# First SwiGLU of a two-layer trunk: one plain block and five pairs, in the order of the inner SwiGLUs

## The chip, the core and the metric

One core of a Trainium2 chip. Its engines run side by side, each through its own instructions in their written order: TensorE (PE; its weight loads are shown apart as PEld) multiplies, VectorE (DVE) and ScalarE (ACT) work element by element, GpSimd (POOL) does that too and issues loads that add to what is already in the buffer ("accumulating loads"), SyncE (SP) issues plain loads. Engines wait for one another by semaphores. SBUF is the memory that all of them read; TensorE writes its sums to PSUM. The metric is the device time of one execution in microseconds (us).

## What is computed

512 tokens of 1024 values go through two layers. Each layer adds half a SwiGLU, then a mixing of attention and convolution, then half a second SwiGLU; a last norm ends it. All in float32. The change is in the very first SwiGLU, the one that begins with the input:

```python
def rms_norm(x, gain):
    inv = lax.rsqrt(jnp.mean(xf * xf, axis=-1, keepdims=True) + NORM_EPS)
    return (xf * inv).astype(x.dtype) * gain

def swiglu(h, w_gate, w_up, w_down):
    return (jax.nn.silu(h @ w_gate) * (h @ w_up)) @ w_down

for l in range(DEPTH):                                   # DEPTH = 2
    x = x + 0.5 * swiglu(rms_norm(x, ffn1_norm[l]), ...)  # w_gate, w_up: 1024 x 2816
    ...                                                   # mixing
    x = x + 0.5 * swiglu(rms_norm(x, ffn2_norm[l]), ...)  # w_down: 2816 x 1024
return rms_norm(x, final_norm)
```

## The kernel before

**Products in three parts.** float32 accuracy comes from splitting each operand into a rounded part and a remainder (hi and lo) and multiplying hi·hi, hi·lo, lo·hi, all summed in PSUM. A weight piece of 512 KB ("unit", tile `raw`) is loaded, ScalarE casts it to `wh` (line 235), VectorE subtracts to get `wl` (line 236). There are eight `raw` tiles and four each of `wh` and `wl`. `need_split` runs the splits up to three units ahead of TensorE and the loads four or more ahead.

**Blocks.** The 2816 hidden columns are 11 blocks of 256. A block can be done *plain*: gate and up for it, 96 products of 128x512. Two blocks can be done as a *pair* by Strassen-Winograd's scheme with seven products in place of eight (`winograd2`): with the tokens cut in four quarters b11, b12, b21, b22 (by halves of the model width and of the tokens), the operands are b11, b21, t2, t3, t1, t4, b22 in this order (table `CHAINS`), where t3 = b12 - b22, t2 = t3 - b11, t1 = b11 - b12, t4 = t2 + b21. Each comes with its combination of weights: a11, a12, s2 = a11 + s1, s3, s1, a22, s4. s1 and s3 are sums of two pieces, made by an accumulating load on GpSimd (line 230); s2 and s4 are added on VectorE (lines 266 and 291). A pair is 168 products. Its results come out turned (tokens by columns), are cut into 16-bit planes by ScalarE, turned back by transposing loads and put together again. A *single* block ("u", `winograd`, line 1162 for its products) is done by the same scheme on half-width products, 168 of 128x256. Down projections are plain for one block ("d", 48 products) or shared over four or five blocks by the same scheme ("s").

**Stages.** A SwiGLU is a list of stages. The first one had its own list: plain blocks 0 and 1, down of 0, pair 2 and 3, down of 1, pairs 4/5, 6/7, 8/9, single 10, shared down of 2 to 5, shared down of 6 to 10. The three inner ones: plain block 0, pair 1/2, down of 0, pairs 3/4, 5/6, 7/8, 9/10, shared down of 3 to 6, down of 1, shared down of 7 to 10 and 2.

**The start.** The first SwiGLU has no norm ahead of it that could be hidden. `First.take` turns the tokens and multiplies them by the gain only; the plain block is computed from these unscaled tokens (`h`), and the scale of each token, `inv`, comes in at the gate (lines 1029 and 1031), when its sums of squares are done. Meanwhile `copy_x` keeps the turned tokens unsplit in `xs`; `First.scale` (line 552, eight VectorE steps) multiplies them by gain and `inv`, and `Seven` makes the pairs' operands from them: adds on VectorE (lines 745 to 751), then a split. Those were spread over plain block 1 and the first down stage.

**Order.** The engines' instructions stand in the order in which the code issues them, apart from what a scheduler moves by priorities; `tc.issue_after` and `behind` hold an instruction behind another. Each engine keeps its order at run time: an instruction that waits holds up everything behind it.

Of the kernel before, what the change touches and what calls it, by code (L numbers as in the profile page):

```python
# [39 lines left out]
)  # L40
LAST = INNER[:-3] + (("s", (1, 3, None)), ("s", (5, 7, None)), ("d", (9, 10)))
# [30 lines left out]
PAIRS = ((0, 1), (2, 3), (4, 5), (6, 7), (8, 9))  # L72
THREES = ((0, 1, 2), (3, 4, 10), (5, 6, 8), (7, 9, 13), (11, 12, 14))
# [9 lines left out]
def trunk_kernel(  # L83
# [161 lines left out]
    def need_split(g):  # L245
        while state["split"] <= min(g, len(order) - 1):
# [6 lines left out]
            elif isinstance(what, tuple):  # L253
# [3 lines left out]
                if at is PAIRS:  # L257
# [10 lines left out]
            else:  # L268

                need_raw(u + 4 + LOAD_AHEAD)  # L270
                a11, a12, s1, s3, a22 = (raw_of.get(u + i) for i in range(5))
                if what == "s2":
                    nc.vector.tensor_add(a11, a11, s1)
                if what == "s4":
                    nc.vector.tensor_add(a11, a11, a12)
                raw = {"a11": a11, "a12": a12, "s2": a11, "s3": s3, "s1": s1, "a22": a22, "s4": a11}[what]
                if what == FORMS[-1]:
                    for i in range(5):
                        del raw_of[u + i]
# [136 lines left out]
    def plan():  # L416
# [5 lines left out]
        def up(wg, wu, b):  # L422
            top, low = ((w, k, KC // 2, 2 * b * P, 2 * P) for w, k in ((wu, 0), (wu, KC // 2)))
            first = (wg, 0, KC // 2, 2 * b * P, 2 * P)
            u = add_unit(first)
            add_unit((wg, KC // 2, KC // 2, 2 * b * P, 2 * P))
            add_unit(top, low)
            add_unit(top, first)
            add_unit(low)
            order.extend((u, what) for what in FORMS)  # L430

        def seven(at, how, wide=2):
# [4 lines left out]
            place = PAIRS if wide == 2 else THREES_EARLY if how == "early" else THREES  # L437
            for n in range(5 * wide):
# [5 lines left out]
        def ffn(wg, wu, wd, stages):  # L444
            for what, b in stages:
# [7 lines left out]
                if what == "u":  # L453
                    up(wg, wu, b)
                if what == "w":
                    seven(
                        lambda o, j, h: ((wg, wu)[o], KC // 2 * j + 2 * h, 2, 2 * b * P, S), None
# [53 lines left out]
    class First:  # L511


        def __init__(self):
            self.h = [None] * KC
            self.inv = None
            self.xs = [g8(f"xs_{n}", F32, (P, KC // 2, S)) for n in range(2)]

        def take(self, c, src):

            g = par[:, c : c + 1]
            if c % 2 == 0:
                self.pair = both(f"h_{c}", shape=(P, 2, 2, S))
            hi, lo = (t[:, c % 2, :] for t in self.pair)
            self.h[c] = (hi, lo)
# [22 lines left out]
        def scale(self):  # L548

            for c in range(KC):  # L550
                x_ = self.xs[c // 4][:, c % 4, :]
                nc.vector.scalar_tensor_tensor(
                    x_, x_, par[:, c : c + 1], self.inv, op0=ALU.mult, op1=ALU.mult
                )
            self.seven = Seven(self.xs, room_stock, "0")
# [1270 lines left out]
```

## Time and profile before

| | |
|---|---|
| Time, median of 3 | 1633.95 us (1630.48 to 1635.71) |
| The profiled execution | 1633.97 us, of which 1632.2 us from its first to its last instruction (the span) |
| Busy in the span | TensorE 1621.6, VectorE 1315.4, ScalarE 1151.2, GpSimd 203.6 us |
| HBM read | 266.10 MB, 164 GB/s over the span |
| DMA queues' packets | 49.1% of 16 engines' span for the plain loads, 30.1% for GpSimd's |

The page counts an engine as busy while one of its instructions runs. The chain of waits is followed back from the last instruction to whatever released each one. Views of single instructions give the start, the duration, engine and line, what is written and read, and in brackets the idle time ahead of it and what ended it. Products run through the array in a pipeline: their rows last 0.39 us, but they follow one another at 0.2267 us (24 of 128x512 in 5.44 us), and it is this pace that counts.

### The profile page before, as it was taken

The page shows a single profiled execution, that of the slowest core. Times are in us where ns is not written, and L with a number is a line of the kernel's source. Part 1 is how long each engine was busy: PE and PEld are TensorE (multiplying, and loading weights), DVE is VectorE, ACT ScalarE, POOL GpSimd, SP SyncE. Part 2 cuts the span into 40 slices and gives each one's busy share as a digit, 9 for nine tenths or more (in the row PEclk, how much of TensorE's full clock was granted, in tenths as well). Part 3 has the DMA queues.
Part 4 walks back from the last instruction along what each step waited for, and adds up shares of the span by engine and source line. Part 5 has one row for each costly group of instructions (what it writes and reads, how often), then busy time and mean ns, then how long its engine had stood idle before and what let it go on. Part 6 is the DMA issues. An engine that isn't in the chain of part 4 may idle for free.

```text
span 1632.2 us, 21149 instructions
## 1 busy us (share of the span) xinstructions
PE 1621.6 (99%) x7526; PEld 1351.2 (83%) x7526; DVE 1315.4 (81%) x1764; ACT 1151.2 (71%) x1632; POOL 203.6 (12%) x184
## 2 busy tenths in 40 slices
PE   9999999999999999999999999999999999999998
PEld 6888888798888888888888888888988888888886
DVE  7987779977898867698888677988678987778894
ACT  6456777668967667785676777856697775778764
POOL 0011111200111111111101111111002101111111
PEclk9999999999999999999999999999999999999999
DMA  8379999943695779899857899998258857899991
GB/s 253 88 201 208 226 218 238 243 132 78 170 217 130 206 190 223 214 223 280 203 125 207 206 219 219 222 275 199 65 110 223 184 131 196 211 220 232 219 270 56
DMA packets 298702, 315.48 MB, mean 193 GB/s; under 512 B 117316, under 2 KB 181348, under 8 KB 298596
## 3 DMA queue, kind: packets, MB, share of 16 engines
q1 hardware_dynamic: 253188, 230.88, 49.1%
q0 software_dynamic: 44704, 82.59, 30.1%
q8 instruction: 59, 0.97, 0.2%
q10 hardware_dynamic: 704, 0.66, 0.1%
q14 instruction: 47, 0.39, 0.1%
HBM read 266.10 MB, written 2.10 MB: 164 GB/s over the span
## 4 chain that ended last, share of the span: by engine, by line
PE 97%; DVE 1%; DMA 1%; ACT 0%; issue 0%; SPq 0%; ACTq 0%; DVEq 0%
PE x L947 25%; PE y L947 13%; PE x_s L947 10%; PE w L947 6%; PE y_s L947 5%; PE up L1109 4%; PE acc L327 4%; PE acc L328 4%; PE acc L330 4%; PE down L394 4%; PE w_s L947 2%; PE acc L371 2%; PE x_m L947 2%; PE y_m L947 1%; PE z_s L947 1%; PE xt L671 1%
## 5 line engine op out<-in xcount | busy, mean ns | idle before, releaser
L236 DVE TENSOR_TENSOR wl<-raw,wh 128x1024 fp32r<-128x1024 f32 (+2 forms) x510 | 607.0, 1196 | 215.0 <-ACT wh L235 211.0
L235 ACT CAST wh<-raw 128x1024 fp32r<-128x1024 f32 (+2 forms) x510 | 520.2, 1026 | 298.7 <-PE y L947 38.5
L947 PE MATMUL y<-wh,ft 128*128 128x512 f32 x608 | 187.3, 389 | 0.0
L947 PE MATMUL x<-wh,ft 128*128 128x512 f32 x608 | 187.3, 389 | 0.0
L947 PE MATMUL x<-wh,fb 128*128 128x512 f32 x608 | 187.3, 389 | 0.0
L947 PEld LDWEIGHTS x<-wh,fb 128*128 128x128 f32 x608 | 114.2, 188 | 23.6
L947 PEld LDWEIGHTS y<-wh,ft 128*128 128x128 f32 x608 | 114.2, 188 | 23.6
L947 PEld LDWEIGHTS x<-wh,ft 128*128 128x128 f32 x608 | 114.2, 188 | 23.6
L947 PE MATMUL y<-wl,ft 128*128 128x512 f32 x304 | 118.3, 389 | 0.0
L947 PE MATMUL x<-wl,fb 128*128 128x512 f32 x304 | 118.3, 389 | 0.0
L947 PE MATMUL x<-wl,ft 128*128 128x512 f32 x304 | 118.3, 389 | 0.0
L230 POOL DMA_DIRECT2D raw<-in_ffn_wu_dram x39 | 47.0, 1212 | 538.6 <-DMA raw<-in_ffn_wu_dram 268.1
L1284 ACT COPY raw_a<-pt 128x1024 uint16<-128x1024 uint16 x76 | 103.3, 1359 | 13.9 <-DMA pt<-pl 13.8
L327 PE MATMUL acc<-hh,wh 128*128 128x512 f32 x240 | 94.1, 392 | 0.0
L947 PE MATMUL w<-wh,fb 128*128 128x512 f32 x304 | 93.6, 389 | 0.0
L328 PE MATMUL acc<-hl,wh 128*128 128x512 f32 x240 | 93.6, 390 | 0.0
L330 PE MATMUL acc<-hh,wl 128*128 128x512 f32 x240 | 93.5, 390 | 0.0
L947 PE MATMUL x_s<-wh,ft_s 128*128 128x512 f32 x256 | 79.0, 390 | 0.0
L947 PE MATMUL y_s<-wh,ft_s 128*128 128x512 f32 x256 | 78.8, 389 | 0.0
L266 DVE TENSOR_TENSOR raw<-raw,raw 128x1024 f32<-128x1024 f32 (+1 forms) x61 | 72.4, 1191 | 7.0 <-DMA raw<-in_ffn_wd_dram 5.4
L230 POOL DMA_DIRECT2D raw<-in_ffn_wd_dram x38 | 43.5, 1146 | 249.5 <-DVE wl L236 146.7
L230 POOL DMA_DIRECT2D raw<-in_ffn_wg_dram x39 | 46.8, 1215 | 219.5 <-DMA raw<-in_ffn_wu_dram 75.1
(385 smaller groups left out, 3478.2 us busy)
## 6 DMA issues: line engine op xcount, KB each, us to landing
raw<-in_ffn_wu_dram SPq DMA_DIRECT2D x120, 512.0 KB, 5.8
raw<-in_ffn_wd_dram SPq DMA_DIRECT2D x98, 512.0 KB, 7.3
raw<-in_ffn_wg_dram SPq DMA_DIRECT2D x80, 512.0 KB, 5.0
raw<-in_ffn_wu_dram POOLq DMA_DIRECT2D x39, 512.0 KB, 8.5
raw<-in_ffn_wg_dram POOLq DMA_DIRECT2D x39, 512.0 KB, 6.1
raw<-in_w_in_dram SPq DMA_DIRECT2D x36, 512.0 KB, 4.7
raw<-in_ffn_wd_dram POOLq DMA_DIRECT2D x32, 512.0 KB, 8.9
raw<-raw POOLq DMA_DIRECT2D x20, 512.0 KB, 8.0
```

The lines of the kernel that those rows point to most:

```text
L230: nc.gpsimd.dma_start(out=r, in_=rows_of(*more), accum_op=ALU.add)
L235: cast = nc.scalar.copy(hi, raw)
L236: state["sub"] = eng.tensor_sub(lo, raw, f32(hi))
L266: nc.vector.tensor_add(a11, a11, s1)
L327: nc.tensor.matmul(acc, hi[:, k, :], rhs[k][0], start=k == first, stop=False)
L328: nc.tensor.matmul(acc, hi[:, k, :], rhs[k][1], start=False, stop=False)
L330: state["product"] = nc.tensor.matmul(acc, lo[:, k, :], rhs[k][0], start=False, stop=k == last)
L371: nc.tensor.matmul(accs[j][:, t * H : (t + 1) * H], w[:, k, :], x_, start=t + k + i == 0, stop=k == KC - 1 and i == 2, skip_group_check=True,)
L394: nc.tensor.matmul(acc, a[:, k, tok], w[:, k, :], start=i + k + n == 0 and fresh[t], stop=i == last and k == 1 and n == 2, skip_group_chec ...
L947: nc.tensor.matmul(accs[u], x_[:, k if h == 2 else 2 * h + k, tok], w[:, k, :], start=start and h + k + i == 0, stop=h == last and k == wi ...
L1109: nc.tensor.matmul(accs[t], x_[:, tok], w[:, k, :], start=j + k + i == 0, stop=j == 3 and k == 1 and i == 2,)
L1284: nc.scalar.copy(room.rearrange("p c (n z) -> p c z n", z=2)[:, :, z, :], turned[0][:, NT * z + 2 * c : NT * z + 2 * c + 2, :],)
```

## The change

The first SwiGLU takes the inner ones' list of stages: one plain block, then pairs 1/2, 3/4, 5/6, 7/8, 9/10, with the down stages as there. Plain block 1 and the single block 10 become parts of pairs. The pairs take tokens that carry the gain but not the scale: `copy_x` multiplies by the gain, `First.scale` is gone, and the scale of a token, now one number per partition because a pair's results have tokens on partitions, comes in as `y` at the Silu and at the product of gate and up. The operands b11, b21 and b22 are slices of the plain block's own hi and lo tiles, and t1 goes into the fourth slice, that of b12. The adds for t3, t2, t1 and t4 go to GpSimd. In the first pair the units are loaded in another order (`PAIRS_FIRST`), s3 is added on VectorE rather than by a load, and t3, t1 and t4 are made after its steps 0, 1 and 2. The tables of attention biases (`late`) are made after the down stage of block 0 instead of block 1.

```diff
-FIRST = (
-    ("p", 0), ("p", 1), ("d", (0,)), ("w", 2), ("d", (1,)), ("w", 4), ("w", 6), ("w", 8), ("u", 10),
-    ("s", (2, 4, None)), ("s", (6, 8, 10)),
-)
 INNER = (
     ("p", 0), ("w", 1), ("d", (0,)), ("w", 3), ("w", 5), ("w", 7), ("w", 9), ("s", (3, 5, None)),
     ("d", (1,)), ("s", (7, 9, 2)),
 )
+FIRST = INNER[:1] + INNER[1:]
 PAIRS = ((0, 1), (2, 3), (4, 5), (6, 7), (8, 9))
+PAIRS_FIRST = ((0, 1), (4, 5), (2, 3), (6, 7), (8, 9))
...
                 if what == "s2":
                     late = state["late"] if h else None
                     late = state["sub"].ins if h == 2 else late
+                    late = state["gate"].ins if how == "first" else late
                     with tc.issue_after(late) if late else nullcontext():
                         nc.vector.tensor_add(a11, a11, s1)
...
                 if what == "s2" if early else what == "s3":
-                    if how:
+                    if how not in (None, "first"):
                         nc.gpsimd.dma_start(out=a12, in_=a11, accum_op=ALU.add)
                     else:
                         nc.vector.tensor_add(a12, a12, a11)
...
     class First:
...
+            self.y = const.tile([P, NT], F32, name="y")
             self.xs = [g8(f"xs_{n}", F32, (P, KC // 2, S)) for n in range(2)]
+            hs = [
+                [
+                    xpool.tile([P, KC // 2, S], F32R, tag="xf", bufs=8, name=f"h{n}_{o}")
+                    for n in "hl"
+                ]
+                for o in range(2)
+            ]
+            self.h = [tuple(p[:, k, :] for p in hs[o]) for o in range(2) for k in range(4)]
+            self.seven = Seven(self.xs, room_g8, "0", eng=nc.gpsimd)
+            places = {
+                f"b{o + 1}{t + 1}": tuple(p[:, :, t * H : (t + 1) * H] for p in hs[o])
+                for o in range(2)
+                for t in range(2)
+            }
+            self.seven.places["t1"] = places.pop("b12")
+            self.forms.update(places)
...
-        def scale(self):
-            for c in range(KC):
-                x_ = self.xs[c // 4][:, c % 4, :]
-                nc.vector.scalar_tensor_tensor(
-                    x_, x_, par[:, c : c + 1], self.inv, op0=ALU.mult, op1=ALU.mult
-                )
...
             if fresh:
-                nc.vector.tensor_sub(sums[0], b12, b22)
+                self.eng.tensor_sub(sums[0], b12, b22)
             if what == "t2":
-                nc.vector.tensor_sub(sums[1], sums[0], b11)
+                self.eng.tensor_sub(sums[1], sums[0], b11)
             if what == "t1":
-                nc.vector.tensor_sub(b12, b11, b12)
+                self.eng.tensor_sub(b12, b11, b12)
             if what == "t4":
-                nc.vector.tensor_add(sums[1], sums[1], b21)
+                self.eng.tensor_add(sums[1], sums[1], b21)
...
+            eng.tensor_scalar(x_, tps[c], g, None, op0=ALU.mult)
...
+        def forms_on(step):
+            names = {0: ("t3",), 1: ("t1",), 2: ("t4",)}.get(step, ())
+            with behind(state["cast"], state["sub"]):
+                norm.make(*names)
...
+            accs = norm.groups(4, opening)
+            gate(accs[0])
+            gate(accs[1])
+            up(0, accs[2])
+            up(1, accs[3])
+            norm.make("t2")
...
+            def silu(t, src):
+                nc.scalar.activation(
+                    gates[t], src, AF.Silu, scale=1.0 if norm.y is None else by(t)
+                )
+            def times(t):
+                if norm.y is None:
+                    nc.vector.tensor_mul(ups[t], ups[t], gates[t])
+                else:
+                    nc.vector.scalar_tensor_tensor(
+                        ups[t], ups[t], by(t), gates[t], op0=ALU.mult, op1=ALU.mult
+                    )
...
-            if b == (1,) and late:
+            if b == (0,) and late:
                 late()
```

How the order of the instructions moves is shown at two places, both behind the first plain block.

GpSimd, its first instructions after the constants, before (units 12, 13, 16, 17 are weights of pairs 2/3):

```order
L503 MEMSET eps_93 128x1
L230 DMA raw_12_485<-in_ffn1_wu_dram 128x2x512
L230 DMA raw_13_524<-in_ffn1_wu_dram 128x2x512
L230 DMA raw_16_577<-in_ffn1_wg_dram 128x2x512
L230 DMA raw_17_580<-in_ffn1_wg_dram 128x2x512
```

and in the changed kernel (units 8 to 11 are s1 and s3 of pair 1/2; `sums` holds t3 and t2, later t4; `xs` the tokens):

```order
L479 MEMSET eps_93 128x1
L228 DMA raw_8_348<-in_ffn1_wu_dram 128x2x512
L228 DMA raw_9_351<-in_ffn1_wu_dram 128x2x512
L228 DMA raw_10_354<-in_ffn1_wg_dram 128x2x512
L228 DMA raw_11_361<-in_ffn1_wg_dram 128x2x512
L727 TENSOR_TENSOR sums_0_413<-xs_0_96,xs_1_97 128x1024
L729 TENSOR_TENSOR sums_0_413<-sums_0_413,xs_0_96 128x1024
L731 TENSOR_TENSOR xs_0_96<-xs_0_96 128x4x256
L733 TENSOR_TENSOR sums_0_413<-sums_0_413,xs_1_97 128x1024
L228 DMA raw_18_653<-in_ffn1_wu_dram 128x2x512
```

Four adds are new on GpSimd, behind the four accumulating loads of the first pair; the fourth of them waits for VectorE's split of t2 (`ft2`).

VectorE, from the first gate of plain block 0 on, before (`fb` is a split operand, `xs` the tokens that are scaled):

```order
L1029 TENSOR_TENSOR gate_0_0_390<-acc_160,inv 128x512
L1029 TENSOR_TENSOR gate_0_1_394<-acc_200,inv 128x512
L552 SCALAR_TENSOR_TENSOR xs_95<-xs_95,par,inv 128x512 x3
L1031 TENSOR_TENSOR gate_0_0_390<-gate_0_0_390,inv 128x512
L1031 TENSOR_TENSOR gate_0_1_394<-gate_0_1_394,inv 128x512
L552 SCALAR_TENSOR_TENSOR xs_95<-xs_95,par,inv 128x512
L552 SCALAR_TENSOR_TENSOR xs_96<-xs_96,par,inv 128x512 x4
L1038 TENSOR_TENSOR gate_0_0_390<-acc_243,gate_0_0_390 128x512
L1038 TENSOR_TENSOR gate_0_1_394<-acc_360,gate_0_1_394 128x512
L236 TENSOR_TENSOR wl_450<-raw_315,wh_449 128x1024
```

and in the changed kernel, after the same two gates by `inv` of line 1029 (now 1017) and 1031 (now 1019) and the two by `acc`:

```order
L234 TENSOR_TENSOR wl_7_440<-raw_7_316,wh_7_439 128x1024
L234 TENSOR_TENSOR a_0_0_331<-gate_0_0_0_398,a_0_0_331 128x512
L234 TENSOR_TENSOR a_0_0_331<-gate_0_0_1_402,a_0_0_331 128x512
L264 TENSOR_TENSOR raw_4_127<-raw_4_127,raw_8_348 128x1024
L234 TENSOR_TENSOR ft2_0_412<-sums_0_413,ft2_0_412 128x1024
L234 TENSOR_TENSOR ft3_0_459<-sums_0_413,ft3_0_459 128x1024
L234 TENSOR_TENSOR wl_8_468<-raw_4_127,wh_8_467 128x1024
L264 TENSOR_TENSOR raw_5_312<-raw_5_312,raw_9_351 128x1024
L1173 TENSOR_TENSOR gate_0_1_0_502<-w_0_1_0_462,p1_0_1_0_455 128x512
L1173 TENSOR_TENSOR gate_0_1_1_505<-w_0_1_1_463,p1_0_1_1_457 128x512
L234 TENSOR_TENSOR wl_9_487<-raw_5_312,wh_9_486 128x1024
```

The scalings are gone, and the first pair's weights and operands follow at once: wl_8 and wl_9 are the two halves of s2, which meet t2 in the pair's third step. Behind them come the add of raw_4 into raw_6, the split of t1 (`hl_0`) and wl_10 and wl_11, the halves of s3.

More of the change, by code (lines that the diff above doesn't have):

```diff
@@ L437, in seven @@
             place = PAIRS if wide == 2 else THREES_EARLY if how == "early" else THREES
+            place = PAIRS_FIRST if how == "first" else place
             for n in range(5 * wide):
@@ L452, in ffn @@
                         order.append((u, None))
-                if what == "u":
-                    up(wg, wu, b)
                 if what == "w":
                     seven(
-                        lambda o, j, h: ((wg, wu)[o], KC // 2 * j + 2 * h, 2, 2 * b * P, S), None
+                        lambda o, j, h: ((wg, wu)[o], KC // 2 * j + 2 * h, 2, 2 * b * P, S),
+                        "first" if stages is FIRST and b == 1 else None,
                     )
@@ L719, in make @@
                     continue
-                hi, lo = both(f"f{what}_{self.name}")
+                hi, lo = self.places.get(what) or both(f"f{what}_{self.name}")
                 self.forms[what] = (hi, lo)
@@ L757, in room_g8 @@
         return t[:, 0], t[:, 1]
-    def room_stock(name):
-        return [stock(f"sum{n}_{name}", shape=(P, KC // 2, H)) for n in range(2)]
     def room_form(name):
@@ L1211, in apart @@
             def apart(t):
-                if then == "u" and t > 1:
-                    pending.setdefault("u", []).append(lambda: lay(t))
-                else:
-                    lay(t)
-            def lay(t):
                 planes.append(g2(f"pl_{name}_{t}", U16, (P, 2, S)))
@@ L1271, in winograd2 @@
                             gates[2 + u] = g2(f"gate_{name}_{2 + u}")
[L1272 to L1273 removed]
+                            silu(2 + u, out)
+                            times(2 + u)
                             apart(2 + u)
@@ L1388, in ffn @@
                 )
-            if b == (0,) and first:
-                norm.make("t4", "b22")
-            if b == (1,) and late:
+            if b == (0,) and late:
                 late()
```

148 lines of the change are left out of this document (21 added, 127 removed).

## The prediction

> **What bounds the kernel now.** I read the page's busy shares and its chain of waits first, then the busy time of each engine in chosen stretches, then single instructions.
>
> ```profile
> PE 1621.6 (99%) x7526; PEld 1351.2 (83%) x7526; DVE 1315.4 (81%) x1764; ACT 1151.2 (71%) x1632; POOL 203.6 (12%) x184
> PE 97%; DVE 1%; DMA 1%; ACT 0%; issue 0%; SPq 0%; ACTq 0%; DVEq 0%
> ```
>
> TensorE is busy 1621.6 of 1632.2 us and makes 97% of the chain that ended last. So only two things can move the time: the number of products, and places where TensorE has nothing to multiply. The stretches show both (columns: stretch, its length, then each engine's busy time, clock, DMA share, GB/s).
>
> ```profile
> 34.27:340.84 306.57, 305.70 (x1428) 254.52 (x1428) 256.51 (x303) 201.08 (x262) 41.67 (x37) 1.00 0.85 201
> 34.27:56.20 21.93, 21.93 (x97) 18.14 (x97) 21.79 (x28) 11.13 (x14) 2.18 (x2) 1.00 0.45 96
> 230.28:250.44 20.16, 20.16 (x170) 20.15 (x169) 18.27 (x22) 16.24 (x27) 2.39 (x2) 1.00 0.97 163
> 521.20:559.28 38.08, 38.08 (x169) 31.54 (x168) 32.47 (x35) 27.30 (x39) 2.38 (x2) 1.00 0.67 187
> 521.20:821.17 299.97, 299.92 (x1331) 248.25 (x1330) 242.44 (x271) 213.20 (x276) 40.17 (x36) 1.00 0.88 215
> ```
>
> The first row is the first SwiGLU from the end of its first plain block to the first product of the mixing: 306.57 us. The last is the same length of program in the next SwiGLU, which already has the order that the change gives the first: from its first pair to the first product of what follows, 299.97 us. The second row is plain block 1 (21.93), the third the single block 10 (20.16), the fourth one pair (38.08, which is 168 products of 0.2267 us). VectorE (third busy column) works 21.79 of 21.93 us behind the first plain block: it has nothing to spare there. The clock is 1.00 throughout.
>
> **The change, part by part. Products.** Removed: 21.93 + 20.16 = 42.09. Added: one pair, 38.08. Gain 4.01 us.
>
> **Order.** 306.57 - 299.97 = 6.60, so another 2.59 us of the first SwiGLU's length is waiting that the inner order does not have. It lies here:
>
> ```profile
> 295.57:325.40 29.83, 28.96 (x122) 22.00 (x120) 26.45 (x36) 18.90 (x28) 7.03 (x7) 1.00 1.05 227
> 294.27 9.38 DMA raw<-in_ffn_wd_dram
> 303.27 0.50 PE L947 MATMUL y_s<-wl,ft_s 128*128 128x512 f32 x1 [0.28 <-DVE wl L236]
> 314.60 0.50 PE L947 MATMUL x_s<-wl,ft_s 128*128 128x512 f32 x1 [0.58 <-DVE wl L236]
> ```
>
> With the single block straight in front of the two last stages, DMA is full (1.05), one accumulating load takes 9.38 us, and weights arrive late at 303 and 314. In the inner order a plain down stage lies between the shared ones, and with a DMA share of 0.88 the stage ran clean. I take all 6.60; if the waiting stays, 4.01.
>
> **The start of the first pair.** This is where the change can lose it again.
>
> ```profile
> 56.37 10.88 PE down L394 x48
> ```
>
> Before, plain block 1 (21.93) and this down stage (10.88) lay between the first block and the first pair; VectorE used them to scale the tokens and form the operands. Now the first pair's products start at 34.27. The operands b11, b21, b22 are free (slices of the plain block's), the eight scalings go, but t2, t3, t1, t4 are formed at once, by four adds that move from VectorE to GpSimd. What VectorE has to do in its new order is priced by these rows:
>
> ```profile
> 31.43 1.29 DVE L1029 TENSOR_TENSOR gate<-acc,inv 128x512 f32<-128x512 f32 x2
> 32.63 2.07 DVE L552 SCALAR_TENSOR_TENSOR xs<-xs,par,inv 128x512 f32<-128x512 f32 x3
> 39.14 1.28 DVE L1038 TENSOR_TENSOR gate<-acc,gate 128x512 f32<-128x512 f32 x2
> 40.34 1.21 DVE L236 TENSOR_TENSOR wl<-raw,wh 128x1024 fp32r<-128x1024 f32 x1
> 41.47 1.28 DVE L236 TENSOR_TENSOR a<-gate,a 128x512 fp32r<-128x512 f32 x2
> 32.71 1.16 ACT L1030 ACTIVATE gate<-gate 128x512 f32<-128x512 f32 x2
> 34.45 1.06 ACT L235 CAST wh<-raw 128x1024 fp32r<-128x1024 f32 x1
> ```
>
> Start to start (40.34 to 41.47) a 1024-wide step costs 1.13, a 512-wide one 0.60. From 33.3, when the first Silu is out, the order lists: two gates by inv, two by acc (to 35.7), the split wl_7 (36.9), two of a (38.1), add raw_8 into raw_4 (39.2), ft2, ft3 (ft2 waits for two GpSimd adds and a cast, so 41.9 and 43.0), wl_8 (44.2), add (45.3), two gate sums (46.5), wl_9 (47.7), add (48.8), hl_0 (50.0), wl_10 (51.1). TensorE wants a split's low part 0.45 us (two products) into its half: wl_8 at 34.27 + 10.88 + 0.45 = 45.6, wl_9 at 48.3, wl_10 at 51.04. So with nothing else in the way this order just meets TensorE, 0.1 us late. Every microsecond more on VectorE is a microsecond of TensorE waiting.
>
> **When GpSimd comes to its adds.** They stand behind four accumulating loads, each of which waits for its plain load.
>
> ```profile
> 19.98 2.40 SPq L212 DMA_DIRECT2D raw<-in_ffn_wd_dram  x2
> 22.62 2.70 SPq L212 DMA_DIRECT2D raw<-in_ffn_wg_dram  x2
> raw<-in_ffn_wg_dram SPq DMA_DIRECT2D x2, 512.0 KB, 7.9
> L230 POOLq EVENT_SEMAPHORE  x2: 17/30/43, 33.2 to 34.5; - x2
> L230 POOL DMA_DIRECT2D raw<-in_ffn_wu_dram x2: 1337/1377/1417, 33.9 to 35.0; - x2
> DMA to landing us min/median/max: 5.8/6.7/7.6
> ```
>
> Units 8 to 11 are loaded at the same places as before, whichever weights they hold: issued from 19.98 to 24.9, 7.9 us to landing, so the first is in at 27.9 and the last at 32.0 to 32.8. GpSimd starts an accumulating load 0.7 us after that (33.2 to 33.9) and holds it 1.4, so its first add starts at 34 to 35, when VectorE is in its most crowded stretch. The accumulated data themselves are not late: the first lands at 28.6 + 7.6 = 36.2, wanted at 38.1; the later ones, at one per 2.9 us (42.6 against 39.7 in the pair of rows above, from the landing times 5.8 and 7.6), at 39, 42 and 45, wanted from 44 to 49.
>
> **What a GpSimd add costs, and whom.** No add of this size is in the trace; the nearest rows are these.
>
> ```profile
> L1770 POOL TENSOR_TENSOR cc<-cc,tap 128x511 f32<-128x511 f32 x8 | 11.3, 1409 | 187.4 <-DVE tap L1767 91.0 <-issue 82.8 <-DVE nm L1595 13.6
> 441.60 1.28 POOL L1770 TENSOR_TENSOR cc<-cc,tap 128x511 f32<-128x511 f32 x1 [2.12 <-DVE tap L1767]
> 452.56 1.77 POOL L1770 TENSOR_TENSOR cc<-cc,tap 128x511 f32<-128x511 f32 x1
> 452.72 2.70 DVE L236 TENSOR_TENSOR wl<-raw,wh 128x1024 fp32r<-128x1024 f32 x1
> 1256.52 1.78 POOL L1770 TENSOR_TENSOR cc<-cc,tap 128x511 f32<-128x511 f32 x1
> 1256.24 3.15 DVE L236 TENSOR_TENSOR wl<-raw,wh 128x1024 fp32r<-128x1024 f32 x1
> 441.35 1.72 DVE L1679 TENSOR_TENSOR m<-o,ol 64x256 f32<-64x256 f32 x4
> ```
>
> Twice a VectorE split, both inputs in SBUF, met a GpSimd add; both times it took 2.70 and 3.15 instead of 1.21 and ended 1.09 us after the add, that is, it did its work only when GpSimd was through (1.77, 1.78). VectorE steps that read one input from PSUM (the four at 441.35) ran on beside an add, undisturbed. So I count an add of 1024 as 2 x 1.29 = 2.58 us in which VectorE can run nothing but its PSUM steps. From below: 2.30 (taking off 0.28 as the add's fixed part, the GpSimd cast of 128x128 on ones_r, below a tenth of that size). From above: 3.06 with the extra 0.48 of the two rows, or 3.56, twice 1.78.
>
> ```profile
> 1.36 0.28 POOL L175 CAST ones_r<-ones 128x128 fp32r<-128x128 f32 x1
> ```
>
> [...]
>
> Put into the order, engines taking turns: add 1 runs 34.55 to 37.13 (the two acc gates beside it); wl_7 to 38.27; add 2 to 40.85; first a to 41.45; add 3 to 44.03; second a, raw add, ft2, ft3 to 48.05; add 4, which waits for ft2, to 50.63; wl_8 to 51.77, 6.2 late; raw add, gate sums, wl_9 to 55.25, 6.9 late; raw add, hl_0, wl_10 to 58.66, **7.6 us late**. From there VectorE has 1.13 to 2.3 us per half of 2.72 and recovers. Low end 7.6 - 4 x 0.28 - 1.2 (the last add beside the two PSUM gate sums) = 5.3; high end 7.6 + 4 x 0.48 = 9.5. I take 7.6, since both meetings in the trace were full exclusions.
>
> **Costed at nothing**, because they lie on engines that catch up: the gain folded into the token copies (same passes over PSUM); Silu with a scale; a product with y in place of a plain one (some 0.06 us each on VectorE); four more transposing and three more 512 KB loads, as the inner SwiGLUs carry them; the bias tables, moved to the first down stage, eight of 0.415 us plus four small ones, about 4.5 us, between x updates and wl_24. With them, counting the order in the same way, wl_24 still comes some 2.5 us before TensorE wants it; with no such cover they would cost up to their 4.5 us.
>
> ```profile
> L936 DVE SCALAR_TENSOR_TENSOR bias<-dist,mask x8: 413/415/417, 118.8 to 121.1; 128x256 bf16<-128x256 f32 x8
> ```
>
> **The sum**, against the profiled execution, 1633.97 us (the median of the three is 1633.95, so no correction): 1633.97 - 6.60 + 7.6 = **1635.0**, with its own range 1632.7 to 1636.9.
>
> **Rivals.** *The adds disturb nothing that counts* (faster): GpSimd waits while VectorE keeps the port, and fits the adds into VectorE's own waits and PSUM steps. For it: six of eight adds in the trace held nobody up. Against: those six met no wide split. Lateness 0.1 instead of 7.6: 1627.5. It stays below the bound while no more than 1.7 us comes back.
>
> *GpSimd keeps the port* (slower): three adds follow one another without a gap for VectorE, each at 3.56. For it: GpSimd won both meetings, once from behind. Against: each add waits on a signal from the one before. The acc gates then no longer run beside add 1, 1.2 more: 7.6 + 4 x 0.98 + 1.2 = 12.7, so 1640.1. This rival is slower than before from 11.5 us on.
>
> *The order does not bring its 2.59*: late weights in the shared stages again, since DMA carries 1.5 MB more than before. Against it: the inner SwiGLU at 0.88 share. 1635.0 + 2.6 = 1637.6.
>
> **How the numbers follow.** About 0.3% (4.9 us) is what a measurement of this kernel can tell from no change: faster is below 1629.0, slower above 1638.9. Forecast 0.42, undisturbed 0.32, GpSimd keeps the port 0.20, order brings less 0.06. The forecast and the last lie within 0.3%; of the faster rival 0.01 does too. Faster 0.31, same 0.49, slower 0.20. The range, 1627.0 to 1640.5, reaches to both outer cases; the forecast's own is given above.
>
> **What would show it.** Right: in the new profile the first pair begins near 34.3 and its first three steps take some 7 us more than 16.3; VectorE's splits there last 2.5 to 4 us each beside GpSimd's adds; the stretch from that pair's fourth step to the mixing runs at 0.2267 us a product, without the waits near 303 and 314. Wrong: splits of 1.2 us beside running adds; waits of TensorE that end with a DMA landing instead of VectorE; waits in the second pair.

## The result, and the profile after

The changed kernel is slower: 1641.97 us in the median of 6 runs (1637.18 to 1642.85) against 1633.06 us for 6 runs of before beside it; ratio 1.0048, 95% interval 1.0032 to 1.0065 (ratios and intervals are worked out from the single runs, so they need not equal the quotient of two medians). The profiled execution took 1642.58 us with a span of 1640.8 us. The page, busy shares and chain of waits:

```profile
PE 1621.7 (99%) x7430; PEld 1345.4 (82%) x7430; DVE 1314.5 (80%) x1743; ACT 1163.4 (71%) x1641; POOL 218.0 (13%) x190
PE 90%; DMA 4%; DVE 3%; ACT 2%; issue 1%; SPq 0%; POOL 0%; DVEq 0%; ACTq 0%; POOLq 0%
```

TensorE shows 96 rows fewer, yet its share of the chain fell from 97% to 90%: 4% now lies with DMA and 3% with VectorE. (Its busy time did not fall, since rows can last longer than their products need: in the first pair they fill 40.15 us where 38.08 are needed.) Busy time by stretch, first of after, then of before (columns as in the prediction: stretch, length, busy time of PE, PEld, DVE, ACT, POOL, clock, DMA share, GB/s):

```profile
34.99:78.72 43.73, 40.15 (x169) 32.73 (x169) 39.34 (x37) 27.28 (x36) 10.04 (x5) 0.96 0.59 163
78.72:280.00 201.28, 201.28 (x890) 166.67 (x888) 158.48 (x174) 148.21 (x180) 25.14 (x22) 1.00 0.89 214
280.00:341.00 61.00, 58.44 (x261) 47.00 (x260) 53.27 (x74) 37.22 (x55) 11.76 (x11) 1.00 0.94 225
```
```profile
280.00:341.00 61.00, 60.13 (x268) 47.97 (x267) 56.58 (x78) 38.37 (x59) 11.84 (x11) 1.00 1.00 245
```

The first pair takes 43.73 us, 5.65 over its 38.08. Then 201.28 us run without a gap. Behind 280.00, where the down stage of block 1 begins, TensorE stands still for 2.56 us in 61; before, with DMA fuller (1.00 against 0.94), 0.87.

The first pair's own rows, GpSimd's first (the start of its accumulating loads and the four adds), then VectorE's, then the two waits of TensorE:

```profile
25.76 2.59 POOL L228 DMA_DIRECT2D raw<-in_ffn_wu_dram  x2 [24.07 <-DMA raw<-in_ffn_wu_dram]
...
30.23 3.02 POOL L727 TENSOR_TENSOR sums<-xs,xs 128x1024 f32<-128x1024 f32 x1
33.32 3.26 POOL L729 TENSOR_TENSOR sums<-sums,xs 128x1024 f32<-128x1024 f32 x1
36.54 2.84 POOL L731 TENSOR_TENSOR xs<-xs 128x1024 f32<-128x1024 f32 x1
45.81 3.26 POOL L733 TENSOR_TENSOR sums<-sums,xs 128x1024 f32<-128x1024 f32 x1 [6.43 <-DVE ft L234]
...
29.66 4.67 DVE L234 TENSOR_TENSOR wl<-raw,wh 128x1024 fp32r<-128x1024 f32 x1
34.26 1.28 DVE L1017 TENSOR_TENSOR gate<-acc,inv 128x512 f32<-128x512 f32 x2
35.63 4.30 DVE L1019 TENSOR_TENSOR gate<-gate,inv 128x512 f32<-128x512 f32 x2
41.05 1.21 DVE L234 TENSOR_TENSOR wl<-raw,wh 128x1024 fp32r<-128x1024 f32 x1
46.80 3.35 DVE L234 TENSOR_TENSOR wl<-raw,wh 128x1024 fp32r<-128x1024 f32 x1
...
34.99 0.50 PE L930 MATMUL x<-wh,hh 128*128 128x512 f32 x1 [1.20 <-DVE gate L1017]
50.21 0.50 PE L930 MATMUL x<-wl,ft 128*128 128x512 f32 x1 [3.57 <-DVE wl L234]
```

With no add beside it (41.05) VectorE's split takes 1.21 us; beside one 4.67 and 3.35. The gates that read PSUM (34.26) run beside add 2 at their usual 1.28 for two; the two that read SBUF alone (35.63) take 4.30 beside the end of add 2 and add 3. TensorE waits 1.20 us ahead of the pair and 3.57 in its third step.

The waits of the shared down stages, and the chain ahead of the first of them (start, length, what):

```profile
292.49 0.70 PE L930 MATMUL x_s<-wh,fb_s 128*128 128x512 f32 x2 [1.45 <-DVE x L1298]
300.53 0.50 PE L930 MATMUL w_s<-wl,fb_s 128*128 128x512 f32 x1 [0.21 <-DVE wl L234]
312.98 0.51 PE L930 MATMUL y_s<-wh,fxt_s 128*128 128x512 f32 x1 [0.36 <-ACT fxt_s L233]
314.01 0.50 PE L930 MATMUL y_s<-wh,fxt_s 128*128 128x512 f32 x1 [0.53 <-DVE fxt_s L234]
```
```profile
271.02 8.33 DMA raw<-in_ffn_wd_dram
...
280.02 10.40 DMA raw<-in_ffn_wd_dram
```
```profile
290.52 1.23 DVE L264 TENSOR_TENSOR raw<-raw,raw 128x1024 f32<-128x1024 f32 x1 [2.74 <-DMA raw<-in_ffn_wd_dram]
291.66 0.68 DVE L1298 SCALAR_TENSOR_TENSOR x<-x_s,x 128x512 f32<-128x512 f32 x1
```

A plain load of 8.33 us is followed by an accumulating load of 10.40 us, which lands at 290.42. VectorE has stood 2.74 us for it, adds the piece, and only then makes the update of x that stands behind it in its order; the first product of the last shared stage waits for that update and comes 1.45 us late.

**Waits by stretch.** Below, a wait is what the starts of two successive products lie apart beyond 0.227 us, where they lie over 0.26 us apart, summed over a stretch. Two profiles of each kernel (us):

| stretch | before | after |
|---|---|---|
| 0 to 95 (start and first pair) | 4.79, 4.07 | 10.81, 10.45 |
| 275 to 345 (shared stages of the first SwiGLU) | 2.63, 3.38 | 4.06, 4.32 |
| 760 to 860 (the same in the second) | 0.67, 1.66 | 1.62, 0.95 |
| 1080 to 1150 (the same in the third) | 0.17, 0.17 | 4.03, 1.66 |

From the mixing on both kernels have the same instructions in the same order on every engine. So the last two rows measure how much one program varies from execution to execution.

### The profile page after: what moved, and what is told of

It reads as the page before. It is cut to its first block, busy times and chain, and to the rows that moved or that the text cites. A ratio compares the mean times of both kernels' runs of the same rounds, so it can differ in the third digit from the quotient of the medians.

```text
span 1640.8 us, 20957 instructions
## 1 busy us (share of the span) xinstructions
PE 1621.7 (99%) x7430; PEld 1345.4 (82%) x7430; DVE 1314.5 (80%) x1743; ACT 1163.4 (71%) x1641; POOL 218.0 (13%) x190
## 4 chain that ended last, share of the span: by engine, by line
PE 90%; DMA 4%; DVE 3%; ACT 2%; issue 1%; SPq 0%; POOL 0%; DVEq 0%; ACTq 0%; POOLq 0%
PE x L930 26%; PE y L930 13%; PE x_s L930 8%; PE w L930 6%; PE up L1085 4%; PE y_s L930 4%; DMA raw<-in_ffn_wd_dram 4%; PE acc L313 3%; PE acc L314 3%; PE acc L316 3%; PE down L380 3%; PE w_s L930 2%; PE acc L357 2%; PE x_m L930 2%; PE y_m L930 1%; PE z_s L930 1%
## 5 line engine op out<-in xcount | busy, mean ns | idle before, releaser
L234 DVE TENSOR_TENSOR wl<-raw,wh 128x1024 fp32r<-128x1024 f32 (+2 forms) x513 | 616.3, 1207 | 222.7 <-ACT wh L233 218.7
L930 PE MATMUL y<-wh,ft 128*128 128x512 f32 x640 | 197.1, 389 | 0.0
L930 PE MATMUL x<-wh,ft 128*128 128x512 f32 x560 | 173.7, 392 | 0.0
L930 PE MATMUL x<-wh,fb 128*128 128x512 f32 x480 | 147.8, 389 | 0.0
L930 PE MATMUL y<-wl,ft 128*128 128x512 f32 x320 | 124.5, 389 | 0.0
L930 PEld LDWEIGHTS x<-wh,ft 128*128 128x128 f32 x560 | 105.8, 189 | 22.1
L930 PE MATMUL x<-wl,ft 128*128 128x512 f32 x280 | 109.6, 391 | 3.6 <-DVE wl L234 3.6
L930 PEld LDWEIGHTS x<-wh,fb 128*128 128x128 f32 x480 | 90.1, 188 | 18.7
L930 PE MATMUL x<-wl,fb 128*128 128x512 f32 x240 | 93.4, 389 | 0.0
L930 PE MATMUL w<-wh,fb 128*128 128x512 f32 x240 | 73.9, 389 | 0.0
```

What stands on the lines that cost most here:

```text
L234: state["sub"] = eng.tensor_sub(lo, raw, f32(hi))
L930: nc.tensor.matmul(accs[u], x_[:, k if h == 2 else 2 * h + k, tok], w[:, k, :], start=start and h + k + i == 0, stop=h == last and k == wi ...
```

## The experiments

### Both kernels again, the adds left out, the adds on VectorE

The first two runs are the two kernels again. `no_adds` leaves out the four adds: t1 to t4 are single quarters of the tokens, and the pairs of the first SwiGLU compute other values.

```diff
 (no_adds, in Seven)
+            if self.eng is nc.gpsimd:
+                return {"b11": b11, "b21": b21, "b22": b22, "t1": b12, "t2": b11, "t3": b12, "t4": b21}[what]
 (adds_dve)
-            self.seven = Seven(self.xs, room_g8, "0", eng=nc.gpsimd)
+            self.seven = Seven(self.xs, room_g8, "0")
```

> The kernel before, unchanged, for a second profile. In the profile of the changed kernel TensorE waited some 4.0 us between 1080 and 1150 us, in the first SwiGLU of the second layer, whose instructions, order and waits are the same in both kernels; in the first profile of the kernel before it waited 0.2 us there. Theory E (an execution's DMA decides): this look can show a wait of 1 to 4 us there too. Theory K (the kernel decides, by what the change shifted in buffers and DMA numbers): 0.2 us again.

> The changed kernel, unchanged, for a second profile and on the same chip as the others. First pair: 43 to 44 us again (38.1 without waits), since its four GpSimd adds stand in the way of VectorE's splits. In the second layer's first SwiGLU: theory E, anything from 0.2 to 4 us of waiting; theory K, 4 us again.

> The changed kernel without the four adds that form t3, t2, t1 and t4 in the first pairs: the splits take single quarters in their place, so the first SwiGLU's pairs compute other values; all else stands. Theory P (the adds on GpSimd shut VectorE's SBUF steps out): the first pair takes 38.1 to 39 us instead of 43.7 and starts within 0.3 us of the end of the plain block instead of 1.3, 6 to 7 us less than the changed kernel. Theory L (the accumulating loads are late for the first pair): the pair stays above 42 us. Theory D (VectorE has too much to do there in any case): 40 to 42 us.

> The changed kernel with the same four adds on VectorE (1.13 us each, 4.5 in all) instead of GpSimd. Theory P: no exclusion any more; by the replay used in the prediction wl_8, wl_9, wl_10 come at 44.8, 48.3 and 50.6 against 45.6, 48.3 and 51.0, so the first pair takes 38.1 to 39 us and the kernel gains 5.5 to 7 us on the changed one, and is 0 to 0.3% faster than the kernel before, depending on the shared stages. Theory D: the pair becomes longer than with the adds on GpSimd, 44 us or more. Theory L: no change, 43 to 44 us.

Measured on one chip, where before had 1634.51 us (22 runs): after again 1638.73, ratio 1.0032 (1.0019 to 1.0045); without the adds 1634.21, 1.0000 (0.9991 to 1.0009); adds on VectorE 1637.66, 1.0019 (1.0009 to 1.0028). The one further execution of before took 1635.04 us.

In the third SwiGLU before again waits 0.17 us, as theory K had it; but after again waits 1.66 where K had 4, so the execution decides (theory E), and the profiles below bear that out.

The first pair without the adds, as a stretch, and two of VectorE's splits in it:

```profile
33.40:78.00 44.60, 44.60 (x197) 36.83 (x197) 39.97 (x45) 30.77 (x41) 4.88 (x5) 1.00 0.72 195
```
```profile
42.76 1.23 DVE L234 TENSOR_TENSOR wl<-raw,wh 128x1024 fp32r<-128x1024 f32 x1
44.49 1.22 DVE L234 TENSOR_TENSOR wl<-raw,wh 128x1024 fp32r<-128x1024 f32 x1
```

TensorE is busy all 44.60 us, the pair starts at the end of the plain block, and the splits take 1.2 us. So the first pair's loss is the adds' doing: 6.15 us by the waits up to 95 us (10.45 in after again, 4.30 here), 4.5 us by the medians (1638.73 to 1634.21), where 6 to 7 were expected. But with them gone the kernel only equals before, although it has 4.0 us of products fewer. The shared stages of the first SwiGLU account for 1.2 us of that (4.17 in this profile, 2.63 and 3.38 in before's two). Those of the second and third wait 2.98 and 2.44 here, more than in before's two profiles, but there both kernels have the same instructions.

With the adds on VectorE the pair is clean too. The kernel is nevertheless 0.2% slower than before, where 0 to 0.3% faster was expected, and its interval overlaps that of after again. TensorE now waits at the end of the first down stage, and more than ever in the shared stage:

```profile
80.76 0.30 DVE L912 CAST dist<-dist_i 128x256 f32<-128x256 int32 x1 [3.56 <-POOL dist_i L910]
...
84.99 0.50 PE L930 MATMUL x<-wh,hh 128*128 128x512 f32 x1 [1.62 <-DVE x L1298]
...
291.94 1.19 PE L930 MATMUL x_s<-wh,fb_s 128*128 128x512 f32 x2 [4.47 <-DVE x L1298]
```

At 80.76 VectorE had stood 3.56 us for the index table of the attention biases, which GpSimd makes (at 79.90) behind two accumulating loads (at 76.71 and 79.15), and what stands behind it in VectorE's order, the update of x that TensorE waits for at 84.99 included, came late.

### Why the shared stages wait: the tiles of b11 and b21

In the first SwiGLU b11 and t1 are slices of one pair of tiles, b21 and b22 of another. A tile comes free when its last reader is done: b11's not after step 0 of the last pair but after step 4, where t1 is used, b21's not after step 1 but after step 6 (in hold_inner, below, two such late readers alone make the operands' casts 7.5 and 11 us later). There are eight such tiles (tag `xf`), and the operands of the next stage, the shared down stage, need some of them during that pair. Which of the eight each operand then takes no profile shows. How late the operands come can be read in after's trace (ScalarE's casts to the shared operands b11 and b21, then GpSimd's loads that add one weight piece to another; the first two rows of each are of the first SwiGLU, the others of the second, where the down stage of block 1 starts at 280.00 and 764.03):

```profile
221.60 1.06 ACT L233 CAST fb_s<-raw_a 128x1024 fp32r<-128x1024 f32 x1
228.22 1.05 ACT L233 CAST fb_s<-raw_a 128x1024 fp32r<-128x1024 f32 x1
...
697.01 1.05 ACT L233 CAST fb_s<-raw_a 128x1024 fp32r<-128x1024 f32 x1
701.21 1.05 ACT L233 CAST fb_s<-raw_a 128x1024 fp32r<-128x1024 f32 x1
...
244.76 0.90 POOL L277 DMA_DIRECT2D raw<-raw  x1 [1.54 <-DVE wl L234]
252.08 0.86 POOL L277 DMA_DIRECT2D raw<-raw  x1 [6.42 <-issue]
...
728.00 1.54 POOL L277 DMA_DIRECT2D raw<-raw  x1
730.41 0.86 POOL L277 DMA_DIRECT2D raw<-raw  x1 [0.87 <-PE x_s L930]
```

The casts stand 58.4 and 51.8 us ahead of that down stage in the first SwiGLU, 67.0 and 62.8 in the second; the second addition 27.9 against 33.6 us. VectorE makes its halves of the operands in the same order, so work moved from a stretch with pauses into its fullest one: between 70 and 50 us ahead of that down stage it is busy 12.68 us in the first SwiGLU and 16.66 in the second, in the 40 us after that 40.00 against 37.35. The additions come later too. SyncE's queue waits for them in both SwiGLUs (23.9 and 20.8 us in the 37 us from 55 us ahead on), and the loads behind them are later in turn. Four kernels are to tell this (theory X) from the alternative that full DMA or chance decides (theory R).

```diff
 (hold_inner: before; `hold` is called behind step 4 with b11, behind step 6 with b21)
+            def hold(what, u, behind_it):
+                if u and then == "s" and getattr(norm, "i", 0) == 2:
+                    with tc.issue_after(behind_it.ins):
+                        nc.vector.tensor_copy(
+                            small(f"held_{what}", 1), f32(norm.forms[what][1][:, 0, :1])
+                        )
 (late_down: before)
-    ("p", 0), ("p", 1), ("d", (0,)), ("w", 2), ("d", (1,)), ("w", 4), ("w", 6), ("w", 8), ("u", 10),
-    ("s", (2, 4, None)), ("s", (6, 8, 10)),
+    ("p", 0), ("p", 1), ("d", (0,)), ("w", 2), ("w", 4), ("w", 6), ("w", 8), ("u", 10),
+    ("s", (2, 4, None)), ("d", (1,)), ("s", (6, 8, 10)),
 (t2_slice: after)
-            self.seven.places["t1"] = places.pop("b12")
+            self.seven.places["t2"] = places.pop("b12")
 (combo: after with the adds on VectorE, t2 in the slice, and)
+            if (what, b) == ("w", 5) and late:
+                late()
...
-            if b == (0,) and late:
-                late()
```

> The kernel before, with one thing added in the second SwiGLU only, which has its own tiles for b11 and b21: two copies of one column each, which read b11 behind step 4 and b21 behind step 6 of its last pair, so that these two tiles come free as late as they do in the first SwiGLU of the changed kernel, where b11 and b21 are slices of larger tiles. Theory X (the slices hold their tiles; the operands of the shared down stage, which want those tiles, are formed 8 to 12 us later, in VectorE's crowded stretch, and everything that it feeds slips, the weight loads last): the cast of the shared stage's b11 moves from 67 us ahead of the down stage of block 1 to about 58, and the waits of the shared stages in the second SwiGLU (760 to 860 us) grow from 0.67 and 1.66 in two profiles to 3.5 to 5; the time grows by 2 to 4 us. Theory R (the waits are a matter of full DMA and of the execution; when the tiles come free is nothing): 0.7 to 1.7 us there, and the time of before.

> The kernel before, with only the down stage of block 1 moved between the two shared down stages of the first SwiGLU, as the inner order has it: the order by itself, without the change's tiles. The prediction's order term: the waits in the shared stages (2.63 and 3.38 us in two profiles) go to the inner ones' 0.7 to 1.7, time 1 to 2.6 us shorter. Theory X agrees with that (the operands have tiles of their own here). Theory R, or a plain failure of the order term: 2.6 us of waits or more, as the changed kernel has 4.1 and 4.3.

> The changed kernel, but the fourth slice (that of b12) is taken by t2, which the pairs use at step 2, and not by t1, which they use at step 4; t1 gets a tile of its own. So the two tiles that hold b11 come free after step 2 of the last pair instead of step 4. Theory X: two of the shared stage's operands (b21, t2) are formed one step, some 5 us, earlier, and the waits at 275 to 345 us go from 4.1 and 4.3 to 2 to 3; b11 itself comes no earlier. Theory R: 4.1 to 4.3 as before. The first pair loses its 5.6 us as in the changed kernel, since the four adds stay on GpSimd.

> The changed kernel with three edits: the four adds on VectorE, t2 in the fourth slice, and the bias tables made after pair 5/6 instead of the first down stage, where VectorE stood 3.56 us for GpSimd's index table and TensorE then 1.78 us at 83.0. First pair without waits (0 to 0.2), nothing at 83.0. Theory X: 2 to 3 us in the shared stages (275 to 345), where the adds on VectorE alone had 7.1; time 1629 to 1632, ratio 0.997 to 0.999. Theory R: 4 to 7 us there, ratio 1.000 to 1.002.

| kernel (before: 1634.06, 31 runs) | time, us | ratio, 95% interval | waits in the shared stages |
|---|---|---|---|
| hold_inner | 1637.00 | 1.0011 (0.9995 to 1.0026) | 5.00 (second SwiGLU) |
| late_down | 1633.72 | 0.9992 (0.9978 to 1.0005) | 1.42 (first) |
| t2_slice | 1638.00 | 1.0013 (1.0000 to 1.0025) | 3.68 (first) |
| combo | 1630.23 | 0.9968 (0.9958 to 0.9979) | 0.48 (first) |

**hold_inner.** Rows of it in the second SwiGLU, then the same casts and additions of before; the down stage of block 1 starts at 761.1 and 760.6:

```profile
701.99 1.05 ACT L235 CAST fb_s<-raw_a 128x1024 fp32r<-128x1024 f32 x1
710.00 1.04 ACT L235 CAST fb_s<-raw_a 128x1024 fp32r<-128x1024 f32 x1
...
733.75 0.86 POOL L291 DMA_DIRECT2D raw<-raw  x1 [6.38 <-PE w_s L947]
...
774.36 0.70 PE L947 MATMUL x_s<-wh,fb_s 128*128 128x512 f32 x2 [2.24 <-DVE x L1394]
```
```profile
693.98 1.06 ACT L235 CAST fb_s<-raw_a 128x1024 fp32r<-128x1024 f32 x1
698.30 1.04 ACT L235 CAST fb_s<-raw_a 128x1024 fp32r<-128x1024 f32 x1
...
727.76 0.86 POOL L291 DMA_DIRECT2D raw<-raw  x1 [1.71 <-DVE wl L236]
```

Two one-column copies, which do nothing but keep two tiles, make the casts 7.5 and 11 us later against the down stage and the second addition 5.5; the waits grow to 5.00 us where the twelve other profiles of this stage have 0.35 to 2.98. The pattern is that of the first SwiGLU of after. The time is 2.9 us longer in the medians, as expected, but its interval still holds 1. And the 5.00 us are from one profile, of an execution of 1640.61 us, 3.6 over this kernel's median. That the operands come later is shown; that the waits follow from it this run alone does not show.

**late_down.** With the order alone, and tiles of their own, the shared stages wait 1.42 us; the three profiles with the order of before (its own two and hold_inner's) have 2.63, 3.38 and 2.49. So by this one profile the order does bring something, 1.4 us against their mean (2.83). The time, expected to be 1 to 2.6 us shorter, does not show it; the same profile waits 0.98 us between 78.72 and 280, where before has 0.21 and 0.10.

**t2_slice.** The operands came earlier as expected (b21's cast 57.4 us ahead instead of 51.8), the waits only fell to 3.68, where 2 to 3 were expected. And the adds, free to run a little sooner, met another victim, in the plain block (VectorE, GpSimd, TensorE):

```profile
29.20 3.93 DVE L896 TENSOR_TENSOR diag<-ident,yl 128x512 fp32r<-128x512 f32 x1
...
29.76 2.81 POOL L727 TENSOR_TENSOR sums<-xs,xs 128x1024 f32<-128x1024 f32 x1
...
33.19 0.50 PE L534 MATMUL ssq<-diag,ones_r 128*128 128x512 f32 x1 [2.82 <-DVE diag L896]
```

The step at 28.60 just ahead of it, of the same kind, took 0.69 us.

**combo** is faster than both kernels. Its first pair and its shared stages:

```profile
33.40:78.00 44.60, 44.07 (x194) 35.75 (x193) 42.62 (x46) 30.39 (x41) 3.59 (x3) 1.00 0.71 190
274.42:335.00 60.58, 60.55 (x275) 50.02 (x274) 53.33 (x74) 36.36 (x56) 9.52 (x10) 1.00 0.91 216
```

TensorE stands 0.53 us in the first pair (0.87 by the distances of starts), where at most 0.2 was expected; dve_t2 below has 0.54 (0.90) there, while the kernels with the adds on VectorE and t1 in the slice have no wait in the pair.

### The three edits one by one

> The changed kernel with the four adds on VectorE and the bias tables made after pair 5/6; t1 stays in the fourth slice, as the change has it. Against the version with all three edits this takes back the slice alone. Theory X (which operand shares a tile with b11 decides how late the shared stage's operands are): the second accumulation raw<-raw starts 27 to 28 us ahead of the down stage of block 1, and the shared stages of the first SwiGLU (275 to 345) wait 3.5 to 7 us, as with the adds alone (7.14); nothing at 83.0; time 1632 to 1636. Theory R (0.48 us with three edits was a lucky execution): 0.5 to 7, whatever the slice.

> The changed kernel with the four adds on VectorE and t2 in the fourth slice; the bias tables stay at the first down stage. Theory X: raw<-raw starts 32 to 34 us ahead of the down stage of block 1 and the shared stages wait 0.4 to 2.5 us, without the tables' move. The wait near 83.0 (1.78 us, VectorE standing 3.56 us for GpSimd's index table) stays if it comes from the tables' place: 1 to 2.5 us. Time 1631 to 1634. Theory R: 0.5 to 7 us in the shared stages.

> All three edits once more, for its interval and a second profile: 1629.5 to 1631.5, ratio 0.996 to 0.998; waits in the first SwiGLU's shared stages 0.4 to 2 us by theory X, anything up to 4 by theory R; first pair under 1 us.

Before had 1634.70 us here (29 runs). All kernels of this table have the adds on VectorE; those with one edit or none are from the batches above and here:

| | tables at the first down stage | tables after pair 5/6 |
|---|---|---|
| t1 in the slice | adds_dve 1637.66; 1.0019 (1.0009 to 1.0028) | dve_late 1633.47; 0.9995 (0.9983 to 1.0007) |
| t2 in the slice | dve_t2 1631.51; 0.9976 (0.9966 to 0.9986) | combo 1630.23; 0.9968 (0.9958 to 0.9979), again 1630.49; 0.9975 (0.9961 to 0.9990) |

The slice brings 0.4% with the tables at the old place and 0.2 to 0.3% at the new one. Moving the tables brings 0.2% beside the t1 slice; beside the t2 slice the intervals overlap. Contrary to what was expected of dve_t2, no wait came near 83.0 there: VectorE's step on the index table had no wait in that profile. So the tables' place alone does not make the wait of 3.56 us; whether the slice or the one execution of adds_dve did stays open. Its shared stages waited 3.95 us where 0.4 to 2.5 were expected; dve_late waited 4.22, within its 3.5 to 7, combo again 1.71.

What the slice does to the operands shows in every profile: the second addition starts 27.5 to 27.9 us ahead of the down stage of block 1 in the five with t1 in the fourth slice, and 32.6 us ahead in the four with t2.

All profiles together, waits in the shared stages:

| tiles of b11 and b21 | profiles | us |
|---|---|---|
| slices, t1 in the fourth (first SwiGLU) | 5 | 4.06, 4.17, 4.22, 4.32, 7.14 |
| slices, t2 in the fourth (first SwiGLU) | 4 | 0.48, 1.71, 3.68, 3.95 |
| their own, inner order (first SwiGLU, late_down) | 1 | 1.42 |
| their own (second SwiGLU) | 12 | 0.35 to 2.98, median 0.77 |
| their own, but held (second SwiGLU, hold_inner) | 1 | 5.00 |
| their own (third SwiGLU) | 13 | 0.17 to 4.76, median 2.30 |

Holding the tiles puts the waits above all twelve of the second SwiGLU, with the change's tiles (5 of 5) and when it is done there by hand (1 of 1). But the third SwiGLU, with tiles of its own, also reaches 4.03 and 4.76 in two of thirteen, so a single profile proves nothing here. For the t2 slice the profiles alone leave open how much it removes, since two of four have nearly 4 us; the times show that it helps, clearly with the tables at the old place, barely at the new one (of the two measurements of combo, one interval ends below that of dve_late, the other overlaps it).

## Why the prediction was wrong

The forecast was +1.0 us with a range up to 1640.5; the kernel took 1641.97. In the prediction's own terms:

**Products, -4.01: right.** Where nothing disturbs it, the new pair and all that follows run at the old pace (44.60 of 44.60 us without the adds, 201.28 of 201.28 in after). Over the whole program the first profile of after waits 12.8 us more than that of before (22.4 less 9.6), and its span is 8.6 us longer: 4.2 us less of products.

**First pair, +7.6: right in its mechanism, a little too large.** The two profiles of after wait 6.2 us more up to 95 us than the two of before (mean 10.63 less 4.43), within 5.3 to 9.5. The adds shut out VectorE's steps with two SBUF inputs (splits of 4.67 and 3.35 us beside an add, 1.21 without) and leave those that read PSUM alone (1.28 us for two gates, with and without), as assumed; without them the loss is gone. Two sizes were off and partly made up for each other: an add took 2.84 to 3.26 us where 2.58 was taken, and the first began at 30.23 and not between 34 and 35, because the plain loads landed sooner: of the four accumulating loads ahead of the adds the first began at 25.76 and not at 28.6, and the last was through at 30.80 and not between 34 and 35. Three adds were thus over by 39.4, ahead of the worst crowding. The 12.7 us rival is wrong: behind each add one of VectorE's steps got through, so that the split ends 1.08 us after add 1 and the gates 0.55 us after add 3. "The adds disturb nothing" is wrong too.

Starting first did not bring VectorE through first: its rows at 29.66 in after and at 29.20 in t2_slice start 0.57 and 0.56 us ahead of GpSimd's add and still end last, 1.08 and 0.56 us behind it. In the two meetings of before, at 452 and 1256, VectorE's row ends 1.09 us behind the add. What the two engines contend for, the rivals' "port", no row shows.

**Order, -2.59: this is the step that failed.** "In the inner order a plain down stage lies between the shared ones, and with a DMA share of 0.88 the stage ran clean. I take all 6.60". The waits grew from 2.63 and 3.38 to 4.06 and 4.32 us, 1.2 more by their means, 3.8 from the forecast; the prediction's own sign, no waits near 303 and 314, failed with those at 300.53, 312.98 and 314.01. The size of 2.59 was fair: the rows shown for it make 0.86, the distances of starts 2.63. But the step took the length of the second SwiGLU for a property of the order. It was one of the order and of its tiles: there b11 and b21 have tiles of their own. The prediction counted the slices only as what they save (operands that need not be formed), not for how long they keep a tile. The order by itself was worth 1.4 us (late_down, one profile), and the tiles took back more than that: with t1 in the slices all five profiles wait over 4 us, and the times with t2 in the slice are 0.2 to 0.4% shorter. How much of the 4 us is the tiles' doing and how much scatter, single profiles do not settle. The rival "the order does not bring its 2.59" named the right outcome with 0.06, but with the wrong cause: it blamed the extra 1.5 MB, and the stage waits longer at a DMA share of 0.94 than before at 1.00. It also had one execution as its measure: the eleven others of that stage with these tiles wait up to 2.98.

**Costed at nothing.** The gain in the copies, the scale in Silu and the product with y cost nothing to be seen (no waits from 78.72 to 280.00). The bias tables were hidden in after; in one profile with the adds on VectorE they were not.

**The sum.** -4.0 + 6.2 + 1.2 = +3.4 us; the second measurement of after, +4.2 (1638.73 less 1634.51), is near it. The first, +8.9, is not: its profiled execution waited 4.03 us in the third SwiGLU, where before waited 0.17 twice but later profiles of the same instructions anything up to 4.76, and 0.78 us at the very end. That part is scatter from execution to execution, which the prediction had no term for. Why its median came out 3 us above the second's stays open.

## What to carry to other kernels

A slice of a tile saves its copy, and keeps the whole tile until the last reader of any slice (two tiles held that long made the next operands' casts 7.5 and 11 us later in hold_inner): ask who needs that tile next, and what that one's lateness pushes into. A stage that runs clean elsewhere in the same kernel is a promise only where its buffers come free at the same steps, so compare the rows of its first instructions, not only its waits. Work given to an idle engine is not free where its steps and a full engine's shut each other out: up to the end of the first pair the four adds cost TensorE less than 1 us on the full engine, at 1.2 us each, and some 6 us on the idle one, at 2.84 to 3.26 us each.

## What the runs showed that was not expected

One program in one place, the shared stages of the third SwiGLU, waited between 0.17 and 4.76 us in thirteen profiles. That is as much as most edits here are worth, and it is why a single profile could not settle any of these terms.

After the wait of 3.57 us that ended at 50.21 TensorE ran slower for a while. Its rows there:

```profile
51.27 1.06 PE L930 MATMUL x<-wh,ft 128*128 128x512 f32 x2
52.12 0.63 PE L930 MATMUL x<-wl,ft 128*128 128x512 f32 x1
52.55 1.06 PE L930 MATMUL x<-wh,ft 128*128 128x512 f32 x2
```

From 51.27 to 52.55 three products start, one every 0.427 us where 0.227 is usual. The clock granted from 51.20 to 54.60 was 0.50, in the stretch after it, to 78.72, 1.00 again; over the first pair that makes the 0.96 of the stretch above. Seven products ran like that, so this wait cost some 1.4 us more than its own length. After the wait of 4.47 us in adds_dve (at 291.94) seven products likewise stand 0.426 us apart, from 292.94 to 295.92; two waits, of 2.24 us (hold_inner, at 774.36) and 2.82 us (t2_slice, at 33.19), were not followed by such a run. What decides it these runs do not show.
